# The first operands of a decoder block's merge: loaded and split while attention ends, from a pool of their own

## The chip, the core and the metric

The kernel runs on one core of one Trainium2 chip. The metric is the device time of one execution in microseconds (us). Three runs of the kernel before took 1291.13, 1292.53 and 1293.98 us; the median is 1292.53 us. One more execution was recorded by the hardware profiler; all times of single instructions below come from it.

## What is computed

One decoder block with two parallel branches, for 1024 tokens of width 1024, in float32. Cut to what matters here:

```python
h = rms_norm(x) * (1 + scale) + shift
q, k, v, z_a, u, z_b, m_a, m_b = split(h @ w_in)          # eight blocks of 1024 columns
attn   = stick_breaking_attention(q, k, v)                 # 16 heads of 64
p_a    = (attn * silu(z_a)) @ w_branch_a
p_b    = (causal_pool(u, pool_w) * silu(z_b)) @ w_branch_b
merged = sigmoid(m_a) * p_a + sigmoid(m_b) * p_b
y      = x + gate * (merged @ w_out)
return rms_norm(y) * final_gain
```

The weight of key s for query t is sigmoid(z_ts) times the product of 1 - sigmoid(z_tj) over the keys j between them, so the logits z pass through two sigmoids and a running product instead of a softmax.

## The kernel before, in words

**Products.** To keep the precision of float32, each operand is split in two halves of the type fp32r: `hi` is the operand cast to fp32r (on ScalarE, or VectorE), `lo` is what is left, a subtraction (VectorE or GpSimd). A product is three matmuls, hi·hi, hi·lo and lo·hi. One block of results, 128 x 512 in one PSUM bank, is a sum over eight blocks of 128: 24 matmuls of 512 columns.

**Stages.** Norm and the projection u; v (stored to HBM, `v_d`); the pooling branch with p_b (stored to `pb_d`); attention (pool `at`); the merge (pool `fin`). In the attention stage the remaining projections run between the logits: k, q and z_a of each pair of heads, and the gates m_a and m_b, whose sigmoids are stored to `sa_d` and `sb_d` (L173 to L178: a tile `m_sg` with one buffer, its store issued from ScalarE's queue).

**Attention** goes over 8 pairs of heads, and in a pair over 8 units (head, pair of query blocks). The logits z of a unit (two matmuls a piece, L550 and L551 the sigmoids on ScalarE, `om` and `be`, and on VectorE the running product) are computed three units ahead of the rest: then TensorE transposes the weights `be` into `wt` (L576 and L577 split it on ScalarE and VectorE), multiplies with `vv` (`avs`), and L602 and L603 add the halves to `tp`, which is multiplied with silu(z_a) on GpSimd and stored to `ga_d` from SP's queue. So the last logits are through three units before attention ends, and the tiles that only logits need (`kl`, `kh`, `q`, `om`) are not touched after them, but they belong to the pool `at`, which is open to the end.

**The merge** goes over the two halves `sh` of the tokens. `load_ga` (L691) loads the eight 128 x 512 blocks of `ga_d` for a half, through three buffers `gr`, from SP's queue, and splits each (cast L697 on ScalarE, subtraction L698 on VectorE). Then for each of eight column blocks j: the weights `wa` are loaded (512 KB) and split (ScalarE, VectorE), three blocks `s_`, `m_`, `b_` of 256 KB are loaded from `sa_d`, `sb_d` and `pb_d` (two buffers each), m = m·b (L726), `pa` is 24 matmuls of wa and ga, s = pa·s (L733), m = m + s (L734), and m is split into `mhl` (L735; the cast is L114, the subtraction L105, both VectorE). In the first half, L737 also loads one eighth of w_out behind each j (512 KB, two buffers `wor`, cast L705 on ScalarE, subtraction L706 on GpSimd). When all eight are there, the products `o` of mhl and w_out follow for four blocks of 128 tokens, with the gate, the residual and the final norm. ga and mhl of both halves share one tag, `k4`, with 20 buffers of 4 KB a partition.

**What sets the order.** A scheduler places every instruction on its engine by a simulated timeline; only TensorE's work of the attention stage (`pinned`) is kept in the order of the program. Each engine then works through its list in order, and an instruction at the head that waits holds back everything behind it. Loads and stores are issued from SP's queue unless the code says `act.dma_start`: then they stand in ScalarE's list. A pool that opens when another closes may lie on its space, and its tiles then wait for the last use of the old tiles beneath them (`reuse_waits="tile"`). PSUM has two banks `pj` for projections and for `pa`, three `z`, two `tr` and one `av`.

Of the kernel before, what the change touches and what calls it, by code (L numbers as in the profile page):

```python
# [9 lines left out]
F32 = mybir.dt.float32  # L10
# [38 lines left out]
def block_kernel(ctx, tc, a, out):  # L49
# [390 lines left out]

    with pool("at") as at:
        pair = {}

        klz = [at.tile([P, 2, S], F32R, name=f"kl{i}") for i in range(2)]
# [4 lines left out]
        def pair_tiles(p, use):  # L449

            def tile_(tag, shape, dt=F32R):
                return at.tile([P] + shape, dt, tag=tag, bufs=2, name=f"{tag}_{p}")

            if use is use_k:
                pair[p] = dict(kh=tile_("kh", [2, S]), kl=klz[p % 2])
            elif use is use_q:
                pair[p]["q"] = [tile_(f"q{h}", [S]) for h in range(2)]
            elif use is use_za:
                pair[p].update(vv=tile_("vv", [8, 2, 2, HD]), za=tile_("za", [S], F32))
# [67 lines left out]

        unit_rows = {}
        z_tags = cycle(Z_TAGS)

        def z_items(u):
# [4 lines left out]
            for qb in (2 * t, 2 * t + 1):  # L536
                n0 = qb * P
                W = S - n0
                om = at.tile([P, S], F32, tag="om", bufs=2, name=f"om{p}_{h}_{qb}")
# [135 lines left out]
        for p in range(NP):  # L675
            used = 0
            for k in range(8):
                upto = QUANTA[p] * sum(SHARE[:k + 1]) // sum(SHARE)
                step(ahead.get(p * 8 + k, []), p * 8 + k, upto - used)
                used = upto  # L680
        pinned[0] = False
# [3 lines left out]
    with pool("fin") as fin:  # L685
        NK = 20

        def k4(shape, name, dt=F32):
            return fin.tile(shape, dt, tag="k4", bufs=NK, name=name)

        def load_ga(sh):  # L691
            ga = []
            for p in range(NP):
                r_ = fin.tile([P, 512], F32, tag="gr", bufs=3, name=f"gr{sh}_{p}")
                nc.sync.dma_start(r_, ga_d[p][:, sh * 512:sh * 512 + 512])
                g_ = k4([P, 2, 512], f"ga{sh}_{p}", F32R)
                act.copy(g_[:, 0], r_)  # L697
                v.tensor_sub(g_[:, 1], r_, g_[:, 0].bitcast(F32))  # L698
                ga.append(g_)
            return ga  # L700

        def load_wo(kb):
# [3 lines left out]
            gp.tensor_sub(wo[:, 1, kb], wr, wo[:, 0, kb].bitcast(F32))  # L706

        ga = load_ga(0)
# [6 lines left out]
        for sh in range(2):  # L715
            sl = slice(sh * 512, sh * 512 + 512)
            ms = []
            for j in range(KB):
# [109 lines left out]
```

## Time and profile before

| | |
|---|---|
| median of three runs | 1292.53 us |
| the profiled execution | 1294.87 us, its span 1293.2 us |
| mean granted TensorE clock | 0.990 |
| busy: PE, VectorE | 1241.9 us (96%), 804.1 us (62%) |
| busy: ScalarE, GpSimd | 548.1 us (42%), 279.3 us (22%) |
| DMA | 192.48 MB, mean 149 GB/s |

PE is TensorE, PEld its weight loads, DVE VectorE, ACT ScalarE, POOL GpSimd, SP the engine that only issues transfers; a `q` behind the name (SPq, ACTq) means the issuing of a transfer there. Columns of the window table: the window and its length, then busy time and instructions of PE, PEld, DVE, ACT and POOL, the granted clock, the DMA share and GB/s. A row of groups gives the line of the code, engine, operation, output <- inputs, the count, and shortest/median/longest duration in ns with the stretch in which they lie. In rows of a timeline, [5.63 <-DMA ...] is the idle time of the engine ahead of the instruction and what ended it.

The span as a whole says that TensorE is busy 96% of it. The slices of PE's row say where it isn't: the first, and the last few, in which the merge lies.

```profile
PE   6799999989999999999999999999999998889997
DMA  8528995862343411233323223232322237855512
```

### The profile page before, as it was taken

Reading aid. Unit: us, or ns where it says so; the run is one execution under the profiler, and the core shown is the slowest. Engines: PE = TensorE matmul, PEld = TensorE weight load, DVE = VectorE, ACT = ScalarE, POOL = GpSimd, SP = SyncE. Lnnn points to the kernel's source line nnn. Section 1 sums busy time; section 2 is a strip of 40 time slices with the busy share of each in tenths; the row PEclk is TensorE's granted clock in tenths of the full one; section 3 lists DMA queues with packets and bytes.
Section 4 is the critical chain, followed back from the end, with each engine's and each line's share of the span. In section 5 each row is a group of like instructions: output and inputs, shape, how many; then the busy total and the mean of one; then the engine's idle time right before and its main releaser. Section 6 shows DMA issues by size and latency. Waiting matters only on the chain.

```text
span 1293.2 us, 16723 instructions
## 1 busy us (share of the span) xinstructions
PE 1241.9 (96%) x6094; PEld 1035.6 (80%) x6094; DVE 804.1 (62%) x1020; ACT 548.1 (42%) x1029; POOL 279.3 (22%) x397
## 2 busy tenths in 40 slices
PE   6799999989999999999999999999999998889997
PEld 5688888768888888888888888888888887667886
DVE  7915342899611177785877768686776743657654
ACT  4445331231101255565656556565655543312101
POOL 4610000102122332322313122231212211400001
PEclk9899999999999999999999999999999999899999
DMA  8528995862343411233323223232322237855512
GB/s 317 204 98 310 330 343 188 303 225 83 113 146 130 155 42 53 70 114 107 122 77 101 80 98 119 90 122 89 99 72 96 96 107 266 288 186 172 183 65 94
DMA packets 72804, 192.48 MB, mean 149 GB/s; under 512 B 7697, under 2 KB 21009, under 8 KB 70802
## 3 DMA queue, kind: packets, MB, share of 16 engines
q1 hardware_dynamic: 63106, 174.38, 39.4%
q10 hardware_dynamic: 9616, 17.04, 3.9%
q8 instruction: 48, 0.79, 0.2%
q14 instruction: 34, 0.28, 0.1%
HBM read 136.86 MB, written 50.34 MB: 145 GB/s over the span
## 4 chain that ended last, share of the span: by engine, by line
PE 78%; DVE 10%; issue 5%; DMA 4%; ACT 1%; POOL 1%; SPq 0%; POOLq 0%; DVEq 0%; ACTq 0%
PE p L90 30%; PE pb L90 7%; PE v L90 7%; PE avs L90 5%; PE o L90 5%; PE wzb L90 5%; PE z L90 5%; PE wt L90 4%; PE u L90 4%; PE pa L90 4%; DVE acc L234 2%; PE ua L90 1%; PE pool L90 1%; DMA wor<-in_w_out 1%; DVE om L557 1%
## 5 line engine op out<-in xcount | busy, mean ns | idle before, releaser
L90 PE MATMUL p<-hT,w 128*128 128x512 f32 x1920 | 538.2, 401 | 0.0
L90 PEld LDWEIGHTS p<-hT,w 128*128 128x128 f32 x1920 | 335.3, 189 | 45.9 <-issue 0.5
L557 DVE TENSOR_TENSOR_SCAN om<-om 128x512 f32<-128x512 f32 (+7 forms) x128 | 175.7, 1372 | 65.7 <-POOL om L555 41.1
L577 DVE TENSOR_TENSOR wt<-wt,wt 128x512 fp32r<-128x512 f32 (+1 forms) x160 | 101.1, 633 | 66.7 <-ACT wt L576 65.4
L550 ACT ACTIVATE om<-z 128x512 f32<-128x512 f32 (+2 forms) x192 | 94.3, 491 | 112.4 <-PE z L90 109.9
L555 POOL TENSOR_SCALAR_AFFINE_SELECT om<-om 128x128 f32<-128x128 f32 x128 | 62.0, 484 | 354.8 <-ACT om L550 318.1
L576 ACT CAST wt<-wt 128x512 fp32r<-128x512 f32 (+1 forms) x160 | 87.2, 545 | 74.9 <-PE wt L90 71.0
L90 PEld LDWEIGHTS avs<-wt,vv 128*128 128x128 f32 x640 | 96.0, 188 | 18.6 <-DVE tp L603 6.7
L558 DVE TENSOR_TENSOR be<-be,om 128x511 f32<-128x511 f32 (+7 forms) x128 | 102.4, 800 | 11.0
L90 PE MATMUL pa<-ga,wa 128*128 128x512 f32 x384 | 94.6, 402 | 10.9 <-DVE ga L698 3.9
L90 PE MATMUL avs<-wt,vv 128*128 128x256 f32 (+1 forms) x640 | 99.8, 278 | 4.5 <-DVE tp L603 4.5
L90 PEld LDWEIGHTS pa<-ga,wa 128*128 128x128 f32 x384 | 73.4, 194 | 31.0 <-DVE ga L698 5.2
L551 ACT ACTIVATE be<-z 128x512 f32<-128x512 f32 (+2 forms) x192 | 93.5, 487 | 0.0
L90 PE MATMUL wzb<-hT,wzb 128*128 128x512 f32 x384 | 92.2, 396 | 0.0
L90 PE MATMUL o<-wo,mhl 128*128 128x512 f32 (+1 forms) x408 | 89.6, 377 | 2.5 <-DVE mhl L114 2.5
L90 PEld LDWEIGHTS wt<-ident,be 128*128 128x128 f32 x576 | 72.4, 141 | 23.6 <-DVE wt L577 1.7
L90 PE MATMUL wt<-ident,be 128*128 128x128 f32 x576 | 89.1, 272 | 0.8 <-DVE wt L577 0.8
L90 PE MATMUL pb<-gb,wb 128*128 128x512 f32 x384 | 88.1, 391 | 0.0
L90 PE MATMUL v<-wv,hT 128*128 128x512 f32 x384 | 87.2, 389 | 0.0
L90 PEld LDWEIGHTS o<-wo,mhl 128*128 128x128 f32 x408 | 73.3, 188 | 17.3 <-DVE mhl L114 3.3
L90 PEld LDWEIGHTS wzb<-hT,wzb 128*128 128x128 f32 x384 | 73.1, 191 | 16.3 <-DVE zs L400 0.3
L90 PEld LDWEIGHTS pb<-gb,wb 128*128 128x128 f32 x384 | 72.1, 188 | 15.8
(118 smaller groups left out, 1538.9 us busy)
## 6 DMA issues: line engine op xcount, KB each, us to landing
w_raw<-in_w_in SPq DMA_DIRECT2D x40, 512.0 KB, 4.4
l_raw<-in_w_in SPq DMA_DIRECT2D x32, 512.0 KB, 5.5
wl_d<-l_raw SPq DMA_DIRECT2D x32, 512.0 KB, 5.0
w<-wl_d SPq DMA_DIRECT2D x32, 512.0 KB, 3.7
v_d<-vo SPq DMA_DIRECT2D x16, 512.0 KB, 5.3
vv<-v_d SPq DMA_DIRECT2D x8, 1024.0 KB, 5.7
wa_raw<-in_w_branch_a SPq DMA_DIRECT2D x16, 512.0 KB, 4.5
wa<-in_w_mod SPq DMA_DIRECT2D x7, 1024.0 KB, 5.5
```

The costliest lines, as they stand in the source:

```text
L90: ins = op(*args, **kw)
L234: v.scalar_tensor_tensor(acc, wa[:, k], sc[:, k:k + 1], acc, ALU.mult, ALU.add)
L550: act.activation(om[:, b0:b0 + n], zp[:, :n], AF.Sigmoid, scale=-0.125)
L551: act.activation(be[:, b0:b0 + n], zp[:, :n], AF.Sigmoid, scale=0.125)
L555: gp.affine_select(out=tl[:, :P], in_=tl[:, :P], pattern=[[1, P]], compare_op=ALU.is_gt, fill=fill, base=0, channel_multiplier=-1)
L557: v.tensor_tensor_scan(om[:, :W], om[:, :W], om[:, :W], 1.0, ALU.mult, ALU.min)
L558: v.tensor_mul(be[:, 1:W], be[:, 1:W], om[:, :W - 1])
L576: act.copy(wt[:, 0, :off], pt[:, :off])
L577: v.tensor_sub(wt[:, 1, :off], pt[:, :off], wt[:, 0, :off].bitcast(F32))
```

## The change

1. The tiles that only logits need (`kl`, `kh`, `q`, `om`) get a pool of their own, `atz`, on the right side of SBUF. It is closed behind the step that issues the last logits (three units before the end of attention), and a pool `fing` is opened there.
2. At that point `load_ga` is called for seven of the eight blocks of the first half; the loads of the first half are issued from ScalarE's queue, those of the second half from SP's as before. The eighth block follows where all eight stood. `gr` (three buffers) and `ga` (now a tag of its own with 12 buffers) lie in `fing`.
3. mhl gets a tag of its own with eight buffers in `fin`.
4. The subtraction that splits w_out (L706) moves from GpSimd to VectorE.

```diff
+    logits = ExitStack()
+    atz = logits.enter_context(pool("atz", side="right"))
     with pool("at") as at:
         pair = {}
-        klz = [at.tile([P, 2, S], F32R, name=f"kl{i}") for i in range(2)]
+        klz = [atz.tile([P, 2, S], F32R, name=f"kl{i}") for i in range(2)]
...
-            def tile_(tag, shape, dt=F32R):
-                return at.tile([P] + shape, dt, tag=tag, bufs=2, name=f"{tag}_{p}")
+            def tile_(tag, shape, dt=F32R, pl=atz):
+                return pl.tile([P] + shape, dt, tag=tag, bufs=2, name=f"{tag}_{p}")
...
-                pair[p].update(vv=tile_("vv", [8, 2, 2, HD]), za=tile_("za", [S], F32))
+                pair[p].update(vv=tile_("vv", [8, 2, 2, HD], pl=at), za=tile_("za", [S], F32, at))
...
+        def load_ga(sh, ps):
+            ga = []
+            for p in ps:
+                r_ = fing.tile([P, 512], F32, tag="gr", bufs=3, name=f"gr{sh}_{p}")
+                (act if sh == 0 else nc.sync).dma_start(r_, ga_d[p][:, sh * 512:sh * 512 + 512])
+                g_ = fing.tile([P, 2, 512], F32R, tag="ga", bufs=12, name=f"ga{sh}_{p}")
+                act.copy(g_[:, 0], r_)
+                v.tensor_sub(g_[:, 1], r_, g_[:, 0].bitcast(F32))
+                ga.append(g_)
+            return ga
...
-                om = at.tile([P, S], F32, tag="om", bufs=2, name=f"om{p}_{h}_{qb}")
+                om = atz.tile([P, S], F32, tag="om", bufs=2, name=f"om{p}_{h}_{qb}")
...
                 step(ahead.get(p * 8 + k, []), p * 8 + k, upto - used)
                 used = upto
+                if p * 8 + k == max(ahead):
+
+                    logits.close()
+                    fing = ctx.enter_context(pool("fing", side="right"))
+                    ga = load_ga(0, range(NP - 1))
         pinned[0] = False
     with pool("fin") as fin:
-        NK = 20
...
-            gp.tensor_sub(wo[:, 1, kb], wr, wo[:, 0, kb].bitcast(F32))
-
-        ga = load_ga(0)
+            v.tensor_sub(wo[:, 1, kb], wr, wo[:, 0, kb].bitcast(F32))
+
+        ga += load_ga(0, [NP - 1])
...
-                ms.append(split(m_, [P, 512], fin, "k4", NK, v, v, f"mhl{sh}_{j}"))
+                ms.append(split(m_, [P, 512], fin, "mhl", 8, v, v, f"mhl{sh}_{j}"))
...
-                ga = load_ga(1)
+                ga = load_ga(1, range(NP))
```

The change moves instructions in the lists of three engines. The first place is ScalarE's list while attention ends: `wt` is a split of transposed weights, `tp` the copy of an attention result, `m_sg` a gate's sigmoid. Before:

```order
L576 CAST wt_1_1_1_9376<-wt_1_1_1_9372 128x384
L602 COPY tp_1_9386<-avs 64x256
L576 CAST wt_1_1_2_9397<-wt_1_1_2_9392 128x512
L602 COPY tp_3_9416<-avs 64x256
L176 ACTIVATE m_sg_9422<-p_0_9368 128x512
L177 DMA sb_d<-m_sg_9422 128x512
L576 CAST wt_1_1_3_9443<-wt_1_1_3_9438 128x512
L576 CAST wt_1_3_3_9463<-wt_1_3_3_9459 128x384
```

Now the loads of gr_0 to gr_2, the cast of wt_1_1_2, the casts of ga_0 and ga_1, the copy tp_3 and the load of gr_3 come first, in this order, and then:

```order
L536 CAST ga_2_9411<-gr_2_9409 128x512
L176 ACTIVATE m_sg_9464<-p_0_9371 128x512
L534 DMA gr_4_9419<-ga_d 128x512
L177 DMA sb_d<-m_sg_9464 128x512
L536 CAST ga_3_9416<-gr_3_9414 128x512
L534 DMA gr_5_9424<-ga_d 128x512
L536 CAST ga_4_9421<-gr_4_9419 128x512
L589 CAST wt_1_1_3_9485<-wt_1_1_3_9480 128x512
L534 DMA gr_6_9429<-ga_d 128x512
L536 CAST ga_5_9426<-gr_5_9424 128x512
L536 CAST ga_6_9431<-gr_6_9429 128x512
L589 CAST wt_1_3_3_9505<-wt_1_3_3_9501 128x384
```

The last two casts of wt now stand behind five and seven casts of ga and behind the loads between them.

The second place is TensorE's list where the merge begins: `pa_0` and `pa_1` are the products of the first two column blocks. Before, eighteen matmuls of pa_0 with ga_0 to ga_5 and six of pa_1 with ga_0 and ga_1 stood ahead of these rows:

```order
L90 MATMUL pa_1_9716<-ga_2_9560,wa_1_9706 128x512 x3
L90 MATMUL pa_1_9716<-ga_3_9565,wa_1_9706 128x512 x3
L90 MATMUL pa_1_9716<-ga_4_9570,wa_1_9706 128x512 x3
L90 MATMUL pa_1_9716<-ga_5_9575,wa_1_9706 128x512 x3
L90 MATMUL pa_0_9670<-ga_6_9580,wa_0_9660 128x512
L90 MATMUL pa_1_9716<-ga_6_9580,wa_1_9706 128x512
L90 MATMUL pa_0_9670<-ga_6_9580,wa_0_9660 128x512 x2
L90 MATMUL pa_0_9670<-ga_7_9585,wa_0_9660 128x512
L90 MATMUL pa_1_9716<-ga_6_9580,wa_1_9706 128x512 x2
L90 MATMUL pa_1_9716<-ga_7_9585,wa_1_9706 128x512
L90 MATMUL pa_0_9670<-ga_7_9585,wa_0_9660 128x512 x2
```

Now, behind the first twenty-one matmuls of pa_0:

```order
L90 MATMUL pa_0_9677<-ga_7_9592,wa_0_9667 128x512 x3
L90 MATMUL pa_1_9723<-ga_0_9401,wa_1_9713 128x512 x3
L90 MATMUL pa_1_9723<-ga_1_9406,wa_1_9713 128x512 x3
L90 MATMUL pa_1_9723<-ga_2_9411,wa_1_9713 128x512 x3
L90 MATMUL pa_1_9723<-ga_3_9416,wa_1_9713 128x512 x3
L90 MATMUL pa_1_9723<-ga_4_9421,wa_1_9713 128x512 x3
L90 MATMUL pa_1_9723<-ga_5_9426,wa_1_9713 128x512 x3
L90 MATMUL pa_1_9723<-ga_6_9431,wa_1_9713 128x512 x3
L90 MATMUL pa_1_9723<-ga_7_9592,wa_1_9713 128x512 x3
L90 MATMUL pa_2_9769<-ga_0_9401,wa_2_9759 128x512 x2
L90 MATMUL o_0_10076<-wo,mhl_0_9704 128x512 x2
L90 MATMUL o_1_10106<-wo,mhl_0_9704 128x512 x2
```

pa_1 no longer overtakes pa_0's last six matmuls: each product runs through, and the first products o come as early as pa_2.

The third place is VectorE's list in the middle of the merge's first half, around block 4: L726 (now L729) is m·b, L733 (L736) pa·s, L734 (L737) the sum m, L114 and L105 splits. Before:

```order
L726 TENSOR_TENSOR m_4_9849<-m_4_9849,b_4_9851 128x512
L733 TENSOR_TENSOR s_4_9847<-pa_4_9854,s_4_9847 128x512
L726 TENSOR_TENSOR m_5_9895<-m_5_9895,b_5_9897 128x512
L734 TENSOR_TENSOR m_4_9849<-m_4_9849,s_4_9847 128x512
L105 TENSOR_TENSOR wa_6_9936<-wa_6_raw,wa_6_9936 128x1024
L114 CAST mhl_4_9881<-m_4_9849 128x512
L105 TENSOR_TENSOR mhl_4_9881<-m_4_9849,mhl_4_9881 128x512
L733 TENSOR_TENSOR s_5_9893<-pa_5_9900,s_5_9893 128x512
```

Now, with the subtractions of w_out (L709) in it:

```order
L729 TENSOR_TENSOR m_4_9856<-m_4_9856,b_4_9858 128x512
L736 TENSOR_TENSOR s_4_9854<-pa_4_9861,s_4_9854 128x512
L737 TENSOR_TENSOR m_4_9856<-m_4_9856,s_4_9854 128x512
L709 TENSOR_TENSOR wo<-wor_9983,wo 128x1024
L114 CAST mhl_4_9888<-m_4_9856 128x512
L105 TENSOR_TENSOR wa_6_9943<-wa_6_raw,wa_6_9943 128x1024
L105 TENSOR_TENSOR mhl_4_9888<-m_4_9856,mhl_4_9888 128x512
L709 TENSOR_TENSOR wo<-wor_10029,wo 128x1024
L729 TENSOR_TENSOR m_5_9902<-m_5_9902,b_5_9904 128x512
L736 TENSOR_TENSOR s_5_9900<-pa_5_9907,s_5_9900 128x512
```

The product m_5 with b_5 stood ahead of the split of wa_6; it now stands behind it, behind the split of mhl_4 and behind two subtractions of w_out.

More of the change, by code (lines that the diff above doesn't have):

```diff
@@ L680, in block_kernel @@
                 used = upto
+                if p * 8 + k == max(ahead):
+                    logits.close()
+                    fing = ctx.enter_context(pool("fing", side="right"))
+                    ga = load_ga(0, range(NP - 1))
         pinned[0] = False
     with pool("fin") as fin:
-        NK = 20
[L688 to L700, printed above, removed]
         def load_wo(kb):
```

## The prediction

> **What bounds the kernel now.** I read the window table first, then TensorE's timeline, then the chain of waits. In the windows the columns are the window, its length, each engine's busy time with instructions, the granted TensorE clock, the DMA share and GB/s.
>
> ```profile
> 1040.00:1080.00 40.00, 40.00 (x214) 33.95 (x213) 14.23 (x22) 14.89 (x32) 6.26 (x12) 1.00 0.36 124
> 1078.00:1091.46 13.46, 13.46 (x61) 11.13 (x60) 3.72 (x5) 3.89 (x6) 0.00 (x0) 1.00 0.94 317
> 1091.46:1116.19 24.73, 16.95 (x53) 11.29 (x51) 11.15 (x12) 11.28 (x14) 9.85 (x4) 0.86 0.84 307
> 1116.19:1134.76 18.57, 17.07 (x75) 13.85 (x75) 16.56 (x15) 6.20 (x6) 10.03 (x4) 1.00 0.77 260
> 1134.76:1167.28 32.52, 28.42 (x120) 21.91 (x120) 18.95 (x29) 4.72 (x6) 0.00 (x0) 1.00 0.56 180
> 1167.28:1199.09 31.81, 31.81 (x140) 26.36 (x141) 19.82 (x33) 8.17 (x19) 3.23 (x7) 1.00 0.54 177
> ```
>
> TensorE is busy throughout while attention ends (first two rows) and again from 1167.28 on. Only the first half of the merge, 1091.46 to 1167.28, has holes. How much is lost there comes from the timeline (start, duration, instruction, count, idle before it):
>
> ```profile
> 1091.46 2.20 PE L90 MATMUL pa<-ga,wa 128*128 128x512 f32 x9
> 1097.56 8.07 PE L90 MATMUL pa<-ga,wa 128*128 128x512 f32 x26 [2.16 <-DVE ga L698]
> 1167.28 31.81 PE L90 MATMUL o<-wo,mhl 128*128 128x512 f32 x139 [0.74 <-DVE mhl L114]
> 1198.92 16.94 PE L90 MATMUL pa<-ga,wa 128*128 128x512 f32 x74
> ```
>
> 139 products undisturbed take 1198.92 - 1167.28 = 31.64 us, 0.2276 each. The three windows start 52, 74 and 119 products (x53, x75 and x120 each count one that reaches over the edge). At full rate these are 11.8, 16.8 and 27.1 us, so the losses are 24.7 - 11.8 = 12.9 (A), 18.6 - 16.8 = 1.7 (B) and 32.5 - 27.1 = 5.4 us (C): **20.0 us** in all, and no gain of this change can be larger.
>
> A waits for the operands ga:
>
> ```profile
> 1077.97 1.39 SPq L695 DMA_DIRECT2D gr<-ga_d  x3
> 1085.57 4.61 SPq L695 DMA_DIRECT2D gr<-ga_d  x3
> DMA to landing us min/median/max: 2.8/4.5/8.2
> L697 ACT CAST ga<-gr x16: 613/620/622, 1082.2 to 1177.5; 128x512 fp32r<-128x512 f32 x16
> L698 DVE TENSOR_TENSOR ga<-gr,ga x16: 678/683/2430, 1083.5 to 1178.5; 128x512 fp32r<-128x512 f32 x16
> ```
>
> Their loads start at 1077.97, when attention has stored its last block, and the queue then stands 4.6 us in the second three, at a DMA share of 0.94. C is a loop through VectorE, as the chain of waits shows it (start, duration, what):
>
> ```profile
> 1144.89 3.81 DMA m<-sb_d
> 1149.43 0.69 DVE m L734
> 1150.12 1.13 DVE wa L105
> 1151.63 0.70 DVE mhl L105
> 1152.34 0.58 DMA m<-sb_d
> ```
>
> The load of m waits for the split of mhl two blocks back, VectorE waits for that load, and the split of the next weights wa stands behind it. One turn takes 1152.34 - 1144.89 = 7.45 us; 24 products pa and 4 products o need 28 x 0.2276 = 6.4.
>
> **The change part by part.** *Seven of eight ga come early.* Seven loads of 256 KB, seven casts of 0.62 and seven subtractions of 0.68 us move from the merge to 1057-1070, where the DMA share is 0.36, into ScalarE's and VectorE's order; the eighth follows the last block it needs. A's first product then has all its operands. What this puts in the way are ScalarE's casts of wt, behind casts that wait for loads:
>
> ```profile
> 1056.62 0.37 ACT L602 COPY tp<-avs 64x256 f32<-64x256 f32 x1 [0.17 <-PE avs L90]
> 1064.85 0.59 ACT L576 CAST wt<-wt 128x512 fp32r<-128x512 f32 x1 [2.58 <-PE wt L90]
> 1067.73 0.48 ACT L576 CAST wt<-wt 128x384 fp32r<-128x384 f32 x1 [2.29 <-PE wt L90]
> 1070.75 0.64 PE L90 MATMUL avs<-wt,vv 128*128 128x256 f32 x4
> 1075.33 0.57 PE L90 MATMUL avs<-wt,vv 128*128 128x256 f32 x4
> ```
>
> The cast of wt at 1064.85 feeds the avs at 1070.75, that at 1067.73 the avs at 1075.33. I follow the new order with a landing time for every load: the first three loads leave at 1057.0; ga_0 and ga_1 are cast when they land; the fourth leaves after the copy tp behind these casts, the fifth after ga_2 and a sigmoid of 0.60; ga_3 and ga_4 are cast when these land, and then comes the first wt (0.59, and 0.68 on VectorE); the seventh load leaves behind it, and the second wt waits for ga_6. With the shortest landing (2.8) the two wt are ready at 1067.4 and 1071.3: nothing is late. With the median (4.5) they are ready at 1070.8 and 1076.3, 0 and 1.0 us late. With the longest (8.2) they are ready at 1078.2, 7.4 late, and at 1087.5, another 4.7 late. Bounds 0 and 12; I take **0.5**, since at a share of 0.36 the burst's landings are too long, if anything.
>
> *What A waits for next.* PSUM has two banks for p and pa. The second product pa_1 needs the bank that ScalarE's last sigmoid frees, and this sigmoid has one buffer, so it waits until the store before it has landed:
>
> ```profile
> 1089.88 0.60 ACT L176 ACTIVATE m_sg<-p 128x512 f32<-128x512 f32 x1 [5.63 <-DMA sa_d<-m_sg]
> 1091.96 0.33 ACTq L177 DMA_DIRECT2D sb_d<-m_sg  x1
> 1098.60 0.59 ACT L176 ACTIVATE m_sg<-p 128x512 f32<-128x512 f32 x1
> ```
>
> That is done at 1098.60 + 0.59 = 1099.2; pa_0 can now end at 1091.46 + 24 x 0.2276 = 1096.9. The difference, **2.3 us**, stays, hidden before by A's other waits. Bounds: if the store needs the 4.5 us of a median landing, it ends by 1096.5 + 0.6, 0.2 us; with 8.2 us at 1100.8, 3.9 us.
>
> *The granted clock.* Where holes are dense, the clock falls behind them:
>
> ```profile
> 1094.00:1096.00 2.00, 0.50 (x1) 0.19 (x1) 1.65 (x1) 1.88 (x4) 1.82 (x1) 1.00 0.83 307
> 1096.00:1098.00 2.00, 0.44 (x2) 0.40 (x3) 2.00 (x3) 0.36 (x1) 0.00 (x0) 1.00 1.03 415
> 1098.00:1100.00 2.00, 1.87 (x8) 1.19 (x7) 1.31 (x3) 1.19 (x2) 1.22 (x1) 0.77 1.03 420
> 1100.00:1102.00 2.00, 2.00 (x6) 1.61 (x5) 0.00 (x0) 0.00 (x0) 1.53 (x1) 0.50 1.03 412
> 1102.00:1104.00 2.00, 2.00 (x9) 1.58 (x8) 0.00 (x0) 0.00 (x0) 0.00 (x0) 0.88 1.02 408
> ```
>
> After 3.1 us of idleness in 4 us the clocks 0.77, 0.50 and 0.88 lose 2 x (0.23 + 0.50 + 0.12) = 1.7 us. The one hole of 2.3 us that I leave may cost 0 to 1.7; I take **0.8**. The Trainium skill ("TensorE: Matmul & The Clock Gate", "What's actually happening") says that the clock is halved after at least one idle window of about 3.4 us; by it a lone hole of 2.3 us would cost nothing and the sum would be 0.8 us better. Here 0.50 was granted although no single hole between two records was longer than the 2.16 us in the row at 1097.56, so I keep half.
>
> *Output weights split on VectorE.* GpSimd loses eight subtractions, VectorE gains eight of 1024 elements.
>
> ```profile
> L705 ACT CAST wo<-wor x8: 1046/1049/1057, 1092.3 to 1129.9; 128x1024 fp32r<-128x1024 f32 x8
> L706 POOL TENSOR_TENSOR wo<-wor,wo x8: 2355/2428/2757, 1093.5 to 1131.1; 128x1024 fp32r<-128x1024 f32 x8
> DMA to landing us min/median/max: 4.1/5.8/8.9
> L105 DVE TENSOR_TENSOR wa<-wa_raw,wa x16: 1214/1218/3418, 1082.3 to 1238.7; 128x1024 fp32r<-128x1024 f32 x16
> 1120.33 2.89 DVE L105 TENSOR_TENSOR mhl<-m,mhl 128x512 fp32r<-128x512 f32 x1
> 1123.59 0.69 DVE L105 TENSOR_TENSOR mhl<-m,mhl 128x512 fp32r<-128x512 f32 x1
> ```
>
> Eight of 1.22 (the form of wa's row) are 9.8 us more on VectorE. But subtractions that ran beside GpSimd's took longer: mhl 2.89 instead of 0.69 at 1120.33, wa up to 3.42 instead of 1.22. Three such cases give 2.2 us each, and ga, m and the first wa some 1 us apiece; VectorE's total hardly changes. What changes is the order: m_5's product, ahead of the split of wa_6 before, now stands behind it and behind two splits of wo, so in C the load has 5 us of other VectorE work to hide in. Per block VectorE then has 0.69 x 4 + 0.42 + 1.22 x 2 = 5.6 us against TensorE's 6.4. So C's loop opens, and B's long subtractions go. Bounds: all 7.1 us of B and C stay, or none; I take **0.5**, because one place (m_6 ahead of wa_7) keeps the old order.
>
> *Buffers.* mhl has eight own buffers instead of a share in twenty. The second half's mhl needs the first half's products o to be over, and TensorE's order already puts those before pa: 0, at worst one split of 0.69 + 0.42. The pool of the logits lies elsewhere in SBUF, so its first tiles wait for other tiles of the stage before than they did:
>
> ```profile
> 432.74 22.37 PE L90 MATMUL p<-hT,w 128*128 128x512 f32 x96
> ```
>
> These 96 products of p, 22 us without a hole, run before the first logits need q. I cost it at 0; only a wait longer than these 22 us would show, as a hole at 455.
>
> **The sum.** 20.0 - 0.5 - 2.3 - 0.8 - 0.5 = **15.9 us**. The profiled execution took 1294.87 us (span 1293.2), so it would be 1279.0; the median 1292.53 is 2.3 lower, which gives **1276.6**.
>
> **Rivals.** *R1, C's loop stays:* every m load still goes out only after a split of mhl, and VectorE still works in order. Against it stands the new order. 4.9 of C's 5.4 us and 1.7 of B come back: 1283.2. *R2, the transfers bound the merge:* shares near 0.84 and 0.77 in A and B speak for it. The seven loads are 1.84 MB; at the 317 GB/s of 1078-1091 taking them out gains only 5.8 us: 1286.7. Against it, C has holes at a share of 0.56. The Trainium skill ("DMA: Bandwidth & Descriptors", "Issuing engines are not separate DMA queues") states that loads issued from ScalarE run on the same 16 engines and save only issue time; the shares above count all queues together and cannot contradict it. *R3, ScalarE's order stalls attention:* the 12.1 us above, instead of 0.5: 1288.2. For it: one queue, three buffers for gr; against it: the slack of 4.6 and 6.4 us between wt and avs in the rows above. *R4, slower:* VectorE's order now waits for the w_out loads. If the two buffers of wor no longer overlap, one block needs 8.9 (longest landing) + 1.05 (ScalarE's cast of wo) + 1.22 = 11.2 us, the split of wa behind it; eight are 89.4 against the 75.8 us of A to C: 1306. It decides from 9.5 us a block; at the median landing of 5.8 it is 8.1. *R5, the loads don't get forward:* if the freed pool's space is held to the end, only B's 1.7 us go: 1290.8.
>
> **How the numbers follow.** Forecast 0.62, R1 0.16, R2 0.07, R3 0.07, R4 0.05, R5 0.03. The range starts at 1292.5 - 20.0 - 1.5 (the spread of the runs shown) = 1271 and reaches to 1286: over R1, to the edge of R2 and R3, leaving out R4, R5 and half of R2 and R3. The forecast's own range is 1272 to 1281. A change of 0.2% is 2.6 us, about what can be told from none: faster 0.91 (forecast, R1, R2, R3, less 0.01), same 0.04, slower 0.05.
>
> **What would show it.** The early casts of ga should lie between 1060 and 1069, with avs as dense as before; pa_0 and pa_1 should run as two blocks of 24 with one hole of 1 to 4 us; the clock should keep 1.00 but for a few us; VectorE's subtractions should stay under 1.3 us; from pa_2 to the end of pa_7 TensorE should have no hole over 1 us, and the second half should begin 14 to 18 us earlier. I am wrong if holes appear before 1091, if the losses after pa_2 stay above 3 us, or if VectorE waits for wor with TensorE behind it.

## The result and the profile after

The changed kernel took **1276.93 us** (median of 4 runs, 1276.39 to 1278.67; the profiled execution 1276.39), the kernel before 1291.87 us beside it: a ratio of 0.9879, 95% interval 0.9861 to 0.9898. Predicted were 1276.6 us and a range of 1271 to 1286. A second measurement on another occasion (six runs) gave 1278.17 us and 0.9892, interval 0.9868 to 0.9916.

A difference of two profiled executions says less than it seems to. Nothing was changed in the program's first 430 us, yet the first product p of attention starts at 432.74 us in the profile before and at 429.22 in the profile after, and between 429.2 and 433.7 us in the other profiles of this study; run times of one kernel spread by 2 to 9 us. For small differences I therefore compare three stretches of each profile, taken from TensorE's timeline: attention (from that p to the last long block of p), the merge's first half (from there to the first pa of the second half) and the end.

| kernel | attention | merge, first half | end | the three together |
|---|---|---|---|---|
| before | 643.0 | 123.2 | 94.3 | 860.5 |
| change | 642.5 | 107.9 | 95.0 | 845.5 |

So 15.3 us are gone from the merge's first half, 0.5 from attention, 0.8 are lost at the end: 15.0 us in all. The remaining 3.5 us between the two spans (1293.2 and 1274.7) lie in the unchanged start.

TensorE's timeline of the change (start, duration, instruction, count, idle before it):

```profile
1071.75 15.89 PE L90 MATMUL p<-hT,w 128*128 128x512 f32 x69
1089.61 7.39 PE L90 MATMUL pa<-ga,wa 128*128 128x512 f32 x24 [1.97 <-ACT m_sg L176]
1097.27 6.22 PE L90 MATMUL pa<-ga,wa 128*128 128x512 f32 x26 [0.27 <-ACT m_sg L176]
1103.33 1.10 PE L90 MATMUL o<-wo,mhl 128*128 128x512 f32 x4
1143.36 36.47 PE L90 MATMUL o<-wo,mhl 128*128 128x512 f32 x160
1179.67 17.12 PE L90 MATMUL pa<-ga,wa 128*128 128x512 f32 x74
```

pa_0 and pa_1 run as blocks of 24 with their operands at hand; where seven holes stood around 1091 to 1116 before, two are left, of 1.97 and 0.27 us, and both wait for ScalarE's sigmoid m_sg, that is for a PSUM bank. From pa_1 to the second half there is none. The windows of the change (columns as before):

```profile
1090.00:1115.00 25.00, 24.73 (x101) 19.79 (x100) 19.44 (x25) 11.17 (x12) 0.00 (x0) 0.93 1.00 379
1115.00:1134.00 19.00, 19.00 (x84) 15.56 (x84) 15.35 (x21) 5.62 (x6) 0.00 (x0) 1.00 0.81 258
1134.00:1149.00 15.00, 15.00 (x67) 12.25 (x66) 11.40 (x17) 4.50 (x6) 0.00 (x0) 1.00 0.67 210
```

The stage that was bound by its operands is now bound by TensorE, while the DMA share went up to 1.00. What is left is the wait for the bank, and here is its chain in ScalarE's timeline:

```profile
1078.31 0.60 ACT L176 ACTIVATE m_sg<-p 128x512 f32<-128x512 f32 x1
1081.00 0.62 ACT L536 CAST ga<-gr 128x512 fp32r<-128x512 f32 x1 [1.15 <-DMA gr<-ga_d]
1081.01 0.35 ACTq L177 DMA_DIRECT2D sa_d<-m_sg  x1
1088.96 0.60 ACT L176 ACTIVATE m_sg<-p 128x512 f32<-128x512 f32 x1 [7.34 <-DMA sa_d<-m_sg]
1090.85 0.33 ACTq L177 DMA_DIRECT2D sb_d<-m_sg  x1
```

The sigmoid of 1088.96 has to wait for the store that was issued at 1081.01. That store took 8 us, about as long as before, but it was issued 2.1 us after its sigmoid, behind a cast of ga that waited for its load. This cast (like two of the three ahead of 1078.31) is of the second half's ga, which twelve buffers let in early.

### The profile page after: what moved, and what is told of

Read it like the earlier page. It is cut to its first block, busy times and chain, and to the rows that moved or that the text cites. A ratio compares the mean times of both kernels' runs of the same rounds, so it can differ in the third digit from the quotient of the medians.

```text
span 1274.7 us, 16720 instructions
## 1 busy us (share of the span) xinstructions
PE 1235.9 (97%) x6094; PEld 1033.8 (81%) x6094; DVE 801.7 (63%) x1028; ACT 548.2 (43%) x1029; POOL 260.3 (20%) x389
## 4 chain that ended last, share of the span: by engine, by line
PE 50%; issue 5%; DVE 2%; DMA 2%; POOL 1%; ACT 1%; SPq 0%; POOLq 0%; DVEq 0%; ACTq 0%
PE p L90 25%; PE pa L90 7%; PE o L90 6%; PE avs L90 5%; PE z L90 4%; PE wt L90 4%; DMA s<-sa_d 1%; DVE om L570 1%; DMA sb_d<-m_sg 0%; DVE be L571 0%; POOL om L568 0%; DVE wt L590 0%; DMA gr<-ga_d 0%; DVE tp L616 0%; POOL be L568 0%
## 5 line engine op out<-in xcount | busy, mean ns | idle before, releaser
L563 ACT ACTIVATE om<-z 128x512 f32<-128x512 f32 (+2 forms) x192 | 94.3, 491 | 112.5 <-PE z L90 110.8
L90 PEld LDWEIGHTS wzb<-hT,wzb 128*128 128x128 f32 x384 | 72.9, 190 | 15.9
```

The lines of the kernel that those rows point to most:

```text
L90: ins = op(*args, **kw)
L563: act.activation(om[:, b0:b0 + n], zp[:, :n], AF.Sigmoid, scale=-0.125)
```

## The experiments

**Which edit brought the gain: two runs that do one part each.** The change with the subtraction of w_out back on GpSimd (run e1):

```diff
-            v.tensor_sub(wo[:, 1, kb], wr, wo[:, 0, kb].bitcast(F32))
+            gp.tensor_sub(wo[:, 1, kb], wr, wo[:, 0, kb].bitcast(F32))
```

> The change, but the subtraction that splits w_out stays on GpSimd. Theory V (the prediction's third term: losses B and C go because w_out is split on VectorE): the 7.1 us of B and C less the 0.5 counted as left come back, 1276.9 + 6.6 = 1283.5 us. Rival O (the early ga alone reorder VectorE's list: here too the product m_5 with b_5 stands behind the split of wa_6): C's loop stays open; only VectorE's subtractions beside GpSimd's get long again (2.2 us each, hidden if VectorE stays under TensorE's 6.4 us a block), 1277 to 1279 us.

It took 1280.16 us (0.9904, 0.9886 to 0.9922), between the two expectations; its merge took 109.4 us, 1.5 more than the change, and the profile says where. Its TensorE timeline:

```profile
1093.08 5.77 PE L90 MATMUL pa<-ga,wa 128*128 128x512 f32 x24 [1.09 <-ACT m_sg L176]
1101.42 7.89 PE L90 MATMUL pa<-ga,wa 128*128 128x512 f32 x26 [2.57 <-ACT m_sg L176]
1109.15 1.09 PE L90 MATMUL o<-wo,mhl 128*128 128x512 f32 x4
1185.50 17.12 PE L90 MATMUL pa<-ga,wa 128*128 128x512 f32 x74
```

The 1.5 us lie in the holes ahead of pa_0 and pa_1 and the low clock behind (pa_1 and the two matmuls after it, 26 in all, take 7.7 us). From the first o to the second half it needs 1185.50 - 1109.15 = 76.35 us, the change 1179.67 - 1103.33 = 76.34: nothing of C came back, as rival O has it. VectorE's long instructions did:

```profile
1111.35 2.63 DVE L114 CAST mhl<-m 128x512 fp32r<-128x512 f32 x1
1114.02 2.79 DVE L105 TENSOR_TENSOR mhl<-m,mhl 128x512 fp32r<-128x512 f32 x1
1125.31 3.43 DVE L105 TENSOR_TENSOR wa<-wa_raw,wa 128x1024 fp32r<-128x1024 f32 x1
```

GpSimd's subtractions ran beside them, the first two like this:

```profile
1110.95 5.30 POOL L709 TENSOR_TENSOR wo<-wor,wo 128x1024 fp32r<-128x1024 f32 x2 [8.12 <-ACT wo L708]
```

VectorE took 2.63, 2.79 and 3.43 us for what takes 0.42, 0.69 and 1.22 in the change, and TensorE waits for none of them. The Trainium skill ("SBUF — State Buffer", "Who interferes with whom") states that a VectorE instruction with two operands in SBUF contends with a GpSimd instruction that reads SBUF; the subtractions here agree (the cast of 2.63 us has one operand and is not covered by that sentence), but what it costs the kernel is nothing while they are off TensorE's path.

The other half alone, the kernel before with w_out split on VectorE (run e2; the same line, the other way round in the kernel before):

> The kernel before with one edit: w_out is split on VectorE; ga are loaded when attention is over. Theory V: B and C lose 6.6 us less, A's 12.9 stay: 1291.9 - 6.6 = 1285.3 us. Rival O: C's loop stays, since VectorE's list still has the product m_5 with b_5 ahead of the split of wa_6; at best B's 1.7 us go, and eight more subtractions stand in VectorE's list while it splits ga: 1290 to 1294 us.

1288.40 us (0.9966, 0.9953 to 0.9980); merge 119.7 us, 3.5 less than before. Rival O expected at most 1.7 us, theory V 6.6; neither is right. Counted as in the prediction, B's 1.7 us are gone and some 2 of C's 5.4, but C's loop is still there: in VectorE's timeline its turns, from one product m·b to the next, are 7.2, 7.6 and 9.4 us long, against the 6.4 that TensorE needs.

```profile
1135.77 0.69 DVE L726 TENSOR_TENSOR m<-m,b 128x512 f32<-128x512 f32 x1 [2.15 <-issue]
1142.93 0.69 DVE L726 TENSOR_TENSOR m<-m,b 128x512 f32<-128x512 f32 x1 [3.06 <-DMA m<-sb_d]
1150.49 0.69 DVE L726 TENSOR_TENSOR m<-m,b 128x512 f32<-128x512 f32 x1 [3.47 <-issue]
1159.93 0.69 DVE L726 TENSOR_TENSOR m<-m,b 128x512 f32<-128x512 f32 x1 [5.34 <-issue]
```

TensorE has enough in hand to run without a hole from 1121 to 1153; the loop catches it only at the end, with a hole of 2.57 us ahead of the last products o. So what opened C in the change is **the early ga**, not VectorE's new work. How the early ga does it was not tested alone; the lists suggest VectorE's order: with ga out of the way the scheduler puts the product m_5 with b_5 behind the split of wa_6 in e1 as well, while in e2 it still stands ahead of it.

**Is C the loop that the prediction read?** The kernel before with a third buffer for m (run e5):

```diff
-                m_ = fin.tile([P, 512], F32, tag="m_", bufs=2, name=f"m{sh}_{j}")
+                m_ = fin.tile([P, 512], F32, tag="m_", bufs=3, name=f"m{sh}_{j}")
```

> The kernel before with one edit: the block m has three buffers instead of two, so that its load no longer waits for the split of mhl two blocks back. Theory L (C is the loop load of m, VectorE, split of wa, as the prediction read it): C's 5.4 us go and A and B stay, so that the stretch from the end of attention's last avs to the second half's first pa shrinks from 123.2 to about 118 us: 1291.6 - 5.4 = 1286.2 us. Rival (another wait is right behind, on the loads of s or b or on VectorE's own work): at least 3 us of C stay: 1289 us or more.

The merge went from 123.2 to 118.2 us in the profiled execution (1287.8 us), but the 5.0 us are not all C's. Counted as in the prediction (74 + 119 + 139 = 332 products from the start of B to the second half), B loses 0.1 instead of 1.7 us and C 2.0 instead of 5.4. So the loop through m's buffer is confirmed for the larger part of C, and B hung on it too: GpSimd still splits w_out here, VectorE's instructions beside it still take up to 2.9 us, and B is gone all the same. VectorE still waits up to 3.16 us for a load of m in C, but one block ahead of need. The median of twelve runs, 1290.20 us (0.9987, 0.9971 to 1.0003), shows only 1.0 us of the 5.0; how much of the difference is the program's start, these runs don't say.

**Does the place in the program matter, or the space?** The change with all eight ga called where they stood before (run e4):

```diff
-                    ga = load_ga(0, range(NP - 1))
+                    ga = []
...
-        ga += load_ga(0, [NP - 1])
+        ga += load_ga(0, range(NP))
```

> The change with both pools, but all eight loads of ga are called where the kernel before called them, behind attention; the scheduler may place them earlier. Theory P (the space decides, not the place in the program): the scheduler's lists stay nearly those of the change and the loads run while attention ends: 1276.9 us, at most 1 us more. Rival (the call's place decides): the loads start when the last block is stored, as before, and A's 9.8 us that the change won come back: 1286.7 us.

1280.90 us (0.9909, 0.9892 to 0.9926); merge 110.1 us, 2.2 more than the change, which is over the 1 us of theory P and far from the 9.8 of its rival. The scheduler pulled the loads forward by itself, the first to 1056.58: the free space is what the change needed. The rest lies again in the holes ahead of pa_0 and pa_1 (3.06 and 1.38 us); as a second profile of the change has one of 3.08, not all of it need be the place of the call.

**What the holes are made of.** The change, with the last gate's sigmoids in two buffers of their own in the new pool (run e3):

```diff
+        sgp = [(wts, 1)]
...
-                    out_ = sigmoid_out(wts, 1, use[p], f"m{ct}")
+                    out_ = sigmoid_out(*sgp[-1], use[p], f"m{ct}")
...
                     fing = ctx.enter_context(pool("fing", side="right"))
+                    sgp.append((fing, 2))
```

> The change, but the last gate's sigmoids get two buffers of their own in the new pool, so that no sigmoid waits for a store. Reading N (the store's landing is the whole of what is left): the holes of 1.97 and 0.27 us ahead of pa_0 and pa_1 go and with them the 1.7 us of clock behind: 1276.9 - 3.9 = 1273.0 us. Reading W (the next wait is close): pa_0 starts at 1087.6 and would end at 1093.1, but the split of wa_1 ends at 1095.15, behind the product m_1 with b_1 that waits for its load; pa_1 starts 1097.27 - 1095.15 = 2.1 us earlier than now, with a hole of 2 us ahead of it and the clock low behind: 1274.8 to 1276.5 us.

1276.16 us (0.9867, 0.9845 to 0.9889); merge 106.4 us, 1.5 less than the change. Reading W holds: pa_0 follows p without a hole, and the next wait is 7 us further on. TensorE's timeline, and ScalarE's:

```profile
1091.96 5.68 PE L90 MATMUL pa<-ga,wa 128*128 128x512 f32 x24
1099.22 0.74 PE L90 MATMUL pa<-ga,wa 128*128 128x512 f32 x2 [1.58 <-ACT wa L110]
1100.67 10.80 PE L90 MATMUL pa<-ga,wa 128*128 128x512 f32 x46 [0.71 <-DVE wa L105]
```

```profile
1086.91 0.59 ACT L176 ACTIVATE m_sg<-p 128x512 f32<-128x512 f32 x1
1096.26 0.33 ACTq L177 DMA_DIRECT2D sb_d<-m_sg  x1
1096.69 0.60 ACT L176 ACTIVATE m_sg<-p 128x512 f32<-128x512 f32 x1 [9.19 <-DMA s<-sa_d]
1098.12 1.05 ACT L110 CAST wa<-wa_raw 128x1024 fp32r<-128x1024 f32 x1
```

ScalarE stands from 1087.5 to 1096.26 until it may issue a store, and the cast of wa_1, for which pa_1 waits, is behind it. The wait is put down to a load of s, whose data this store has nothing to do with. The program's list of waits says why: the loads and stores of both queues count on eight semaphores (counters that a transfer raises when it has landed), DMAHW0 to DMAHW7, given out in turn, and a transfer that gets one of them waits until the one that used it last has landed. This store got DMAHW1, which the load of s_1 used eight transfers before:

```
L177 DMA sb_d_73<-m63_sg0_9629 128x512 [waits DMAHW1_49,Activation_49]
```

**Which queue loads ga.** The change with the first half's ga loaded from SP's queue (run e7):

```diff
-                (act if sh == 0 else nc.sync).dma_start(r_, ga_d[p][:, sh * 512:sh * 512 + 512])
+                nc.sync.dma_start(r_, ga_d[p][:, sh * 512:sh * 512 + 512])
```

> The change, but the first half's ga are loaded from SP's queue, not ScalarE's. If the loads in ScalarE's list hold up the casts of wt (the third rival of the prediction), avs comes earlier by up to the few tenths of a us that attention lost; the traces show no such loss, so: from the first product p of attention to the last avs 642.5 us as now. What SP's list gets is seven loads ahead of the last weights w_39, which the product p needs some 5 us after they land now: no hole. Expected 1276.9 us, within 1 us; if the holes ahead of pa_0 and pa_1 change (the stores stand on other places among the loads), within 3 us.

1280.87 us (0.9915, 0.9894 to 0.9936); attention 642.8 us, unchanged, so ScalarE's list cost attention nothing; but the merge took 112.3 us, 4.4 more, above the expected 3. pa_0 waits 2.00 us for its bank as in the change, but pa_1 waits 3.73 for the product s with pa_0, that is for pa_0's own bank, and the clock falls behind it. TensorE:

```profile
1093.61 5.79 PE L90 MATMUL pa<-ga,wa 128*128 128x512 f32 x24 [2.00 <-ACT m_sg L176]
1103.12 8.41 PE L90 MATMUL pa<-ga,wa 128*128 128x512 f32 x24 [3.73 <-DVE s L736]
```

SP's queue stands 10.64 us in the seven loads (from 1056.11), but that costs nothing: measured against the start of attention's last long block of p, the weights behind them are issued at the same time as in the change, and the merge's other loads within 0.6 us of it or earlier, apart from two of the second half's ga, 2 us later. What came late is on ScalarE:

```profile
1092.95 0.60 ACT L176 ACTIVATE m_sg<-p 128x512 f32<-128x512 f32 x1 [6.23 <-DMA sa_d<-m_sg]
1097.37 0.33 ACTq L177 DMA_DIRECT2D sb_d<-m_sg  x1
1097.79 1.05 ACT L708 CAST wo<-wor 128x1024 fp32r<-128x1024 f32 x1 [4.24 <-DMA wor<-in_w_out]
1103.35 0.60 ACT L176 ACTIVATE m_sg<-p 128x512 f32<-128x512 f32 x1 [1.67 <-DMA sb_d<-m_sg]
```

The store of sb_d leaves 3.8 us behind its sigmoid's end, 1.3 in the change (1088.96 + 0.60 to 1090.85), and the last sigmoid, which frees pa_1's usual bank, comes behind it. The program's list of waits has the reason of e3 again: with the loads in another queue the semaphores fall to other transfers, and this store now waits for a load of w_out (wor_1, DMAHW5) instead of the load of s_1. No run gave the store another semaphore and left the rest alone.

The Trainium skill ("DMA: Bandwidth & Descriptors", "Issuing engines are not separate DMA queues") states that issuing from several engines saves only the time of issuing. Here the choice of the queue was worth 4.4 us in the profiled merge, by neither bandwidth nor the time of issuing, but by the order of the transfers and by what each has to wait for.

**Why the end got longer.** The matmuls pa of the second half take longer in the change, at a granted clock of 1.00. The addresses differ: ga lay 3488 bytes behind a 4096-byte boundary before and lies 4064 bytes behind one now. The change with padding in the new pool, which moves ga back to 3488, all work in the same order (run e6):

```diff
                     ga = load_ga(0, range(NP - 1))
+                    fing.tile([P, 144], F32, tag="pad", bufs=1, name="pad")
```

> The change with 576 bytes of padding in the new pool, so that ga lie at the same offset from a 4096-byte boundary as in the kernel before (3488 instead of 4064); the order of all work is the same. Theory (position): the matmuls pa take 0.2267 us again, as before, instead of 0.2292: 384 x 0.0025 = 1.0 us less, 1275.9 us, and the row of 48 matmuls pa in the second half shows 10.9 instead of 11.0 to 11.2 us from start to start. Rival (another cause): these rows stay, 1276.9 us.

TensorE's timelines, the change first, then the padded one, each with two rows of 48 matmuls (the rows of o that follow them start at 1209.00 and 1222.05 in the change, at 1209.48 and 1222.18 in the padded one):

```profile
1197.99 11.17 PE L90 MATMUL pa<-ga,wa 128*128 128x512 f32 x48
1210.85 11.36 PE L90 MATMUL pa<-ga,wa 128*128 128x512 f32 x48
```

```profile
1198.60 11.04 PE L90 MATMUL pa<-ga,wa 128*128 128x512 f32 x48
1211.30 11.04 PE L90 MATMUL pa<-ga,wa 128*128 128x512 f32 x48
```

From start to start, 11.01 and 11.20 us become 10.88 and 10.88, the figure of before, and the end takes 94.2 us again. The position theory holds, and in every other run too: the five with the padding have an end of 94.2 to 94.3 us, the six with ga in the change's position one of 95.0 to 95.1. The median (1277.71 us; 0.9888, 0.9863 to 0.9913) can't show 1 us, and this execution's hole ahead of pa_0 was 2.70 us, so that its merge stayed at 107.9.

**A version with all of it.** Two buffers for the last gate's sigmoids, their stores from GpSimd, eight buffers for ga, the padding, and in the first trial the two broadcast vectors of the end loaded while attention ends (run e8; not all lines are shown, the first is against the run with two buffers, the others against the change):

```diff
-                    sgp.append((fing, 2))
+                    sgp.append((fing, 2, gp))
...
-                g_ = fing.tile([P, 2, 512], F32R, tag="ga", bufs=12, name=f"ga{sh}_{p}")
+                g_ = fing.tile([P, 2, 512], F32R, tag="ga", bufs=8, name=f"ga{sh}_{p}")
...
+                    bg = fing.tile([P, D], F32, name="bg")
+                    nc.sync.dma_start(bg, g_d.broadcast_to([P, D]))
+                    fg = fing.tile([P, D], F32, name="fg")
+                    nc.sync.dma_start(fg, a["final_gain"].broadcast_to([P, D]))
```

> The change with what the runs so far name put together: two buffers of their own for the last gate's sigmoids, their stores issued from GpSimd, so that ScalarE's casts do not stand behind a store that may not be issued yet; the two broadcast vectors of the end (1 MB) loaded while attention ends; eight buffers for ga instead of twelve (no early loads of the second half's ga beyond three); the padding. Theory: pa_0 follows the last p without a hole; the product m_1 with b_1, ahead of wa_1's split in VectorE's list, gets its load 1 MB / 410 GB/s = 2.5 us earlier than with two buffers alone, where pa_1 had 2.3 us of holes: none to 0.5 left, the clock stays at 1.00, pa at 0.2267. 1276.2 - 1.8 - 1.0 = 1273.4 us, and with no hole at all 1272.9. Rival (the burst of loads bounds this place whatever the order): the holes stay, 1275.2 us.

The merge took 104.3 us, 3.7 less than the change, and no hole is left ahead of pa_0 and pa_1; but attention took 643.7, 1.2 more. For 0.6 of it TensorE waits for tp, whose copy stands in ScalarE's list behind casts of ga that now get their data later:

```profile
1076.28 0.68 PE L90 MATMUL avs<-wt,vv 128*128 128x256 f32 x4 [0.61 <-DVE tp L617]
```

That is the prediction's third rival in small: it needed another MB of loads. The median was 1278.37 us (0.9896, 0.9875 to 0.9917), no better than the change.

The last four runs went onto one chip: the change again (run e9; merge 108.5 us, one hole of 3.08), and three variants.

> The change itself once more, to be compared with the next three on one chip. By its first measurement 1276.9 us; the stretch from the last avs block to the second half's first pa 107.9 us, what follows 95.0 us. If the start of the program (its first 430 us, where nothing was changed) varies by some us between executions, as the traces so far show (from 429.2 to 433.4 us to the first p of attention), the median may come out 1 to 2 us higher, and these two stretches stay.

In the next (run e10), the two vectors are loaded into w_out's buffers once these are free:

```diff
+                bg = fin.tile([P, D], F32, tag="wor", bufs=2, name="bg")
+                nc.sync.dma_start(bg, g_d.broadcast_to([P, D]))
+                fg = fin.tile([P, D], F32, tag="wor", bufs=2, name="fg")
+                nc.sync.dma_start(fg, a["final_gain"].broadcast_to([P, D]))
                 ga = load_ga(1, range(NP))
```

> The last version (two buffers for the last gate's sigmoids, their stores from GpSimd, eight buffers for ga, padding), but the two broadcast vectors of the end are loaded into the buffers of w_out when these come free, neither while attention ends nor in the burst at the merge's start. Theory: the 0.61 us that avs waited in that version is gone (attention 642.5 to 642.8 us), the merge keeps 104.3 and the end 94.3: 4.4 us below the change on the same chip. Rival (the early loads were what closed the holes): pa_1 gets back the 2.3 us of holes it had with two buffers alone, 2 us below the change.

1276.35 us (0.9867, 0.9847 to 0.9887): attention 642.7, the merge 105.9 (C's loop shows again with holes of 0.93 and 1.04 us at its end), the end 94.2: 3.5 us less than the change beside it in the three stretches, 1.8 in the medians. With a third buffer for m as well (run e11; the diff above):

> As the run before, with three buffers for m. If what is left of C (0.77 us ahead of the last products o of the first half) is the wait of m's load for its buffer, it goes: merge 103.5 us, 5.2 us below the change. If not, as the run before.

1279.84 us (0.9895, 0.9874 to 0.9915), merge 108.6: worse. The buffer that won 5 us in the kernel before lost 2.7 here. In VectorE's list the product m_2 with b_2 now comes ahead of the split of wa_1 and waits for its load, and pa_1 waits with it. VectorE, then TensorE:

```profile
1099.11 0.69 DVE L728 TENSOR_TENSOR m<-m,b 128x512 f32<-128x512 f32 x1 [3.78 <-DMA b<-pb_d]
1100.85 1.22 DVE L105 TENSOR_TENSOR wa<-wa_raw,wa 128x1024 fp32r<-128x1024 f32 x1
```

```profile
1102.12 12.79 PE L90 MATMUL pa<-ga,wa 128*128 128x512 f32 x48 [3.88 <-DVE wa L105]
```

Last, e10 with the second half's ga through the buffers of b, so that none comes early (run e12):

```diff
-                r_ = fing.tile([P, 512], F32, tag="gr", bufs=3, name=f"gr{sh}_{p}")
+                r_ = fing.tile([P, 512], F32, tag="gr", bufs=3, name=f"gr{sh}_{p}") if sh == 0 else fin.tile([P, 512], F32, tag="b_", bufs=2, name=f"gr{sh}_{p}")
```

> As e10_late_gains, with the second half's ga loaded through the buffers of b, so that none of them is loaded before the first half is nearly over. If the burst at the merge's start is what the loads there wait for, 0.8 MB less of it brings them up to 1.9 us earlier, which is worth at most the holes that are left; if the second half's ga come too late, a hole appears ahead of its first pa at about 1180 us. Expected: as e10_late_gains within 1 us.

**1274.51 us** (four runs, 1272.54 to 1276.73; 0.9857, interval 0.9837 to 0.9877), the merge 105.1 us, 0.8 less than without this edit and so within the 1 us expected, the end 94.2. TensorE's timeline, and the window of the 25 us behind the start of pa:

```profile
1091.38 16.48 PE L90 MATMUL pa<-ga,wa 128*128 128x512 f32 x72
```

```profile
1092.00:1117.00 25.00, 25.00 (x112) 20.67 (x112) 19.64 (x24) 11.28 (x12) 0.54 (x1) 1.00 0.96 346
```

72 matmuls in a row at a DMA share of 0.96. It clearly beats the kernel before; against the change beside it (1278.17 us, 0.9892) the medians say 3.7 us and the three stretches 4.2 (842.1 against 846.3), while the two intervals still overlap a little.

## Why the prediction was right, and where it wasn't

The sum had five numbers, 20.0 - 0.5 - 2.3 - 0.8 - 0.5 = 15.9 us. Measured were 15.3 in the merge's first half and 15.0 over all three stretches. A's gain came by the mechanism that was forecast; B and C went as forecast, but through another edit than the one credited, and some of the other terms were off in ways that cancelled, so that the closeness of the sum is in part luck.

- **A's operands** came early as said. Of its 12.9 us the bank and the clock below are left.
- **ScalarE's order (0.5 predicted, 0 measured).** The casts of wt and the products avs that need them, in the change, ScalarE first, then TensorE:

```profile
1063.08 0.58 ACT L589 CAST wt<-wt 128x512 fp32r<-128x512 f32 x1
1066.30 0.47 ACT L589 CAST wt<-wt 128x384 fp32r<-128x384 f32 x1
```

```profile
1066.77 0.64 PE L90 MATMUL avs<-wt,vv 128*128 128x256 f32 x4
1071.35 0.57 PE L90 MATMUL avs<-wt,vv 128*128 128x256 f32 x4
```

  With VectorE's 0.68 and 0.55 the two wt were ready at 1064.5 and 1067.6, 2.3 and 3.8 us ahead of need. The seven early loads took 2.7 to 4.9 us to land, 3.2 in the median, nearer the shortest of the working (2.8) than its median (4.5), as its bounds allowed.
- **The bank (2.3 predicted, 1.97 + 0.27 = 2.24 measured).** The mechanism, one buffer behind a store, is right, and e3 shows it by removing it. The place is wrong: the step took pa_0's bank to come free as before, 1 us ahead of need. It came 2 us late, because the store was issued later against TensorE's work: 1087.64 - 1081.01 = 6.6 us ahead of the last p's end, 9.2 before (1091.46 - 1082.22, the issue in the profile before). What stands ahead of it in ScalarE's list are casts of the second half's ga: two ahead of the sigmoid, beside the eighth of the first half, and one, with a wait of 1.15 us for its load, between the sigmoid and its store. The prediction counted the casts of the first half and overlooked these; no run took them away alone. That the size fits is luck; in the second profile of the change the hole was 3.08 us.
- **The clock (0.8 predicted, 1.7 measured).** This is a term that was mis-sized, by keeping half. The windows behind the hole of 1.97 us:

```profile
1090.00:1092.00 2.00, 2.00 (x8) 1.59 (x7) 0.00 (x0) 0.73 (x1) 0.00 (x0) 0.67 0.99 393
1092.00:1094.00 2.00, 2.00 (x7) 1.51 (x6) 1.81 (x3) 1.89 (x3) 0.00 (x0) 0.50 0.91 332
1094.00:1096.00 2.00, 2.00 (x10) 1.65 (x9) 2.00 (x3) 0.67 (x2) 0.00 (x0) 0.97 1.06 417
```

  2 x (0.33 + 0.50 + 0.03) = 1.7 us. The rule that the prediction cites from the Trainium skill ("TensorE: Matmul & The Clock Gate", "What's actually happening"), by which a lone hole of this length would cost nothing, does not hold here.
- **B and C (0.5 predicted, no hole measured)**, but the step gave the credit to the wrong edit. The split of w_out on VectorE removed VectorE's long subtractions, which cost nothing once ga come early (e1), and did not open C's loop (e2); the early ga did, most likely by the new order of VectorE's list, which the step had named. B did not hang on the long subtractions either: e5 keeps them and loses 0.1 us there. Had the change been the split alone, the same step would have predicted 6.6 us and 3.5 would have come.
- **Buffers at 0**: right. **What no step had**: the matmuls pa are some 0.0025 us slower each with ga in its new position, 0.5 us in the first half and 0.8 at the end (e6).
- First half: 20.0 - 2.24 - 1.7 - 0.5 = 15.6; 15.3 were measured. The 0.3 us between them lie in how the rows count: a row ends some 0.16 us after the time that its matmuls take from start to start (11.17 against 11.01 us in e6's rows), and the idle time counts from the row's end, so each of the two holes cost about 0.16 us more than its row says. The 0.5 us that attention gained are not explained; the other runs with the change gained 0.2 to 0.3, but for e8.

Of the rivals, R1 (C stays) is what e2 shows without the early ga. R2 (transfers bound) fails: the share did rise to 1.00, yet e12, which moves the same bytes in all but some of them later, keeps TensorE busy at a share of 0.96, so it was their order. R3 and R4 did not come; R5 is answered by e4, where the loads went forward even from a late call.

## What to carry to other kernels

Operands that can be loaded early need a place that is free early: a pool of their own for what dies first is the larger part of such a change, and the scheduler does the rest. Before crediting a gain to an edit, undo that edit alone: here the visible relief (short subtractions on VectorE) was worth nothing once the operands came early, and 3.5 us without them, and the same third buffer won 5 us in one version and lost 2.7 in another, since it changes an engine's list. When loads move forward, look at what their casts and issues stand in front of in each list, stores that free a PSUM bank above all, and at which older transfer each of them waits for through a shared semaphore.

## What was not expected of the hardware

**A hole of 2 us can cost 3.7.** Behind holes of 1.97 (change), 2.57 (e1), 2.70 (e6), 3.06 (e4), 3.08 (e9) and 3.88 us (e11) the granted clock falls to about 0.5, and the loss is 1.7 us each time, that is 3.4 us at half speed. It doesn't follow the hole's length alone: in e7 a hole of 2.00 us ahead of pa_0 left the clock at 1.00, in the place where 1.97 us in the change did not, and so did 2.57 us in e2.

Windows finer than those above show what decides. In the merge, the stretch at half speed is 3.41 us long in every trace that has one, or twice that (6.83 us, around the end of e7's hole of 3.73). The two such stretches of the kernel before start 10.24 us apart, at 1099.08 and 1109.32, and those of e2 6.83, at 1106.53 and 1113.36: three and two times 3.41. So the clock seems to be set anew every 3.41 us, at instants that the program does not choose. Reckoned back from its slow stretch in steps of 3.41 us, the window ahead of the fall in the change, and the one in e7 that holds most of the 2.00 us, are these:

```profile
1087.28:1090.69 3.41, 1.44 (x7) 0.92 (x6) 0.69 (x1) 0.60 (x1) 0.00 (x0) 1.00 1.05 395
```

```profile
1091.78:1095.19 3.41, 1.58 (x7) 1.32 (x8) 0.69 (x1) 0.60 (x1) 0.00 (x0) 1.00 1.04 411
```

TensorE is idle for 3.41 - 1.44 = 1.97 us of the first and for 1.83 of the second. Of the windows at full speed in the merge's first half, in the ten traces with a slow stretch, every one with 1.9 us of idleness or more is followed by half speed and none with less than 1.75 is; in between, 1.78 and 1.89 were, 1.83 and 1.86 were not. The 2.57 us of e2 fall into two windows, 0.96 and 1.62. So a rough estimate from these traces is that a window more than about half idle is enough.

The Trainium skill ("TensorE: Matmul & The Clock Gate", "What's actually happening") describes a free-running window of about 3.4 us. The duration of the slow stretch and its dependence on where the hole lies agree with that; that a whole window has to be idle does not.

**The moving operand's position has a price.** 512 columns of ga that start 32 bytes ahead of a 4096-byte boundary take 0.2294 us a matmul (11.01 us for 48), and up to 0.2333 (11.20); 608 bytes ahead of it, 0.2267 (10.88). Which boundary it is, and whether 32 bytes matter or the crossing, was not tried.
